# Seven products for eight in part of the first FFN projection of a hybrid decoder layer, and PSUM as one pool

## The chip, the cores and the metric

One core of a Trainium2 chip. The metric is the device time of one execution, in microseconds; runs of the same kernel on the same chip are compared. Engines are TensorE (PE, with its weight loads as PEld), VectorE (DVE), ScalarE (ACT), GpSimd (POOL) and SyncE (SP), which issues the loads.

## What is computed

One layer of a decoder trunk on 256 rows of width 2048, all in float32: a conditioned norm, one wide input projection, two token mixers (an RG-LRU and a windowed attention), gated output projections, and then the part that matters here:

```python
h2 = modulate(rms_norm(x, norm2_g[l]), sh2, sc2)
gate, up = jnp.split(h2 @ w_ffn_in[l], 2, axis=-1)     # 2048 -> 2 x 5632
x = x + g2 * ((jax.nn.silu(gate) * up) @ w_ffn_out[l]) # 5632 -> 2048
```

## The kernel before, in words

**Precision.** A float32 product is made of three matmuls in a reduced type. Each weight block and each activation is split in a high and a low part, and `mm3` (line 346) issues high by high, high by low and low by high into one PSUM bank. ScalarE makes the high part of a weight block (`do_hi`, line 295, the copy at line 301), VectorE the low part (`do_lo`, line 306, the subtraction at line 313).

**Items.** All projections are one list of `Item`s. A normal item is one load of 128x1024 weights (two k-tiles of 128 by 512 columns) with twelve matmuls of 512 columns: two k-tiles, two blocks of 128 rows, three each. `step(i)` (line 323) fixes the order on every queue by hand: first one stage of each open epilogue (`run_posts`, the list `posts`), then the load of item i+5, the making of item i+4 where its weights are computed and not loaded, the high part of i+3, the low part of i+2, then the item's `before` stages, the matmuls of item i, and side work that fits by a planner's clocks (`run_sides`: the costs `T_PE`, `T_DVE`, `T_ACT`, `T_DMA` in line 69). High parts have four buffers, low parts three, loads five, so the low part of i+2 can start only when the matmuls of item i-1 are done. The last four items (`keep=True`) hold their parts in another pool and are free of that.

**First FFN projection** (`add_slab`, line 352, called at lines 1153 to 1155): for each of 11 slabs of 512 hidden columns, first the gate slab (tiles `fg`), then the factor slab (`fu`), each over 16 k-tiles in eight items, into two banks, one for each block of rows. `gate_f_post` (line 1113) applies SiLU behind the gate slab; `up_f_post` (line 1121) multiplies, turns the result by eight transposes (`turned`, line 887), and splits it in parts for the last projection.

**Last projection** (`seven`, line 1206): for eight pairs of k-tiles (`SEVEN`, line 64) a block product of 2x2 blocks (two blocks of rows, two k-tiles, two blocks of columns) is made of seven products where eight would do it plainly. Sums of activation blocks (`f_sum`) and differences of weight blocks (`first` and `second`, lines 1234 and 1243) are needed; four sums of products (`p`, `q`, `r`, `u`) are shared by the pairs and added up once at the end (`combined`, line 1259). It runs in two sweeps; a pair is four items: two loads and two items whose weights VectorE makes.

**PSUM.** Two pools of four banks: `ps_w` for slabs, `ps_m` for the rest, the latter counted by `used["m"]`.

**Around them.** `second_norm` (line 1029) makes the parts of h2 ahead of the first FFN projection, and its `rest` (line 1084) finishes them as an epilogue, one stage for each item. `ada_rows` (line 606) is side work: the last modulation, 32 multiply-adds on VectorE (line 623) into the tile `pa`, and four copies through PSUM (line 629). Behind the last item `finish_first` and `finish_last` (lines 1343 and 1372) end the kernel.

Of the kernel before, what the change touches and what calls it, by code (L numbers as in the profile page):

```python
# [9 lines left out]
F32 = mybir.dt.float32  # L10
# [53 lines left out]
SEVEN = tuple(range(6, 36, 4))  # L64
EARLY = NH - 2 * N_HOLD
# [7 lines left out]
def hybrid_layer(  # L73
# [12 lines left out]
    ps_w = ctx.enter_context(tc.tile_pool(name="ps_w", bufs=4, space=PSUM))  # L86
    ps_m = ctx.enter_context(tc.tile_pool(name="ps_m", bufs=4, space=PSUM))
# [178 lines left out]
    class Item:  # L266


        def __init__(self, src, cols, mm, post=None, keep=False, weight=1, used=None, before=()):
            self.src, self.cols, self.mm, self.post, self.keep, self.weight = src, cols, mm, post, keep, weight  # L270

            self.used, self.before = used or cols, list(before)
# [22 lines left out]
    def do_hi(i):  # L295
        cols, keep = items[i].used, items[i].keep
# [4 lines left out]
        nc.scalar.copy(hi[:, :cols], live[i][0][:, :cols])  # L301
        clock["act"] = max(clock["act"], live[i][3])
        charge(0, cols * T_ACT)
        live[i][1], live[i][3] = hi, clock["act"]

    def do_lo(i):
        cols, keep = items[i].used, items[i].keep
# [5 lines left out]
        nc.vector.tensor_tensor(lo[:, :cols], raw[:, :cols], f32(hi[:, :cols]), op=ALU.subtract)  # L313
        clock["dve"] = max(clock["dve"], live[i][3])
        charge(cols * T_DVE, 0)
# [7 lines left out]
    def step(i):  # L323
        it = items[i]
        run_posts()
# [3 lines left out]
        upto("lo", do_lo, i + N_LO)  # L329
        for stage in it.before:  # L330
            charge(*stage())
# [20 lines left out]
    def add_slab(slab, name, act, k0, k1, post, in_rows=False, before=None, late=0):  # L352
# [25 lines left out]
        for a in range(k0, k1, 2):  # L378
# [3 lines left out]
            ))  # L382

# [643 lines left out]
    h2 = {}  # L1027

    def second_norm(banks):
# [54 lines left out]
        def rest():  # L1084
            turn(7)
            for p in range(NK // 2):
# [5 lines left out]
                yield 1.33, 1.4  # L1092

# [27 lines left out]
    def up_f_post(s):  # L1121
        def post(banks):
# [7 lines left out]
            if 4 * s + 2 not in SEVEN:  # L1130
                fh, fl = b4(f"fh{s}", F32R), b4(f"fl{s}", F32R)
                yield from parts_of(pts, fh, fl)
                f_hi[s], f_lo[s] = fh, fl
                return

            fc, fs = b4(f"fc{s}", F32R, (2, 2, S)), b4(f"fs{s}", F32, (8, P))
            nc.scalar.copy(fc[:, 0], pts[0])
            nc.scalar.copy(fs[:, 0:2, :], pts[1][:, :, 0:P])
            nc.scalar.copy(fs[:, 2, :], pts[1][:, 1, P:])
            yield 0, 1.3  # L1140
            nc.vector.tensor_tensor(fc[:, 1], pts[0], f32(fc[:, 0]), op=ALU.subtract)
            a11, a12, a22, a21 = fs[:, 0, :], fs[:, 1, :], fs[:, 2, :], pts[1][:, 0, P:]
            s1, s2, s3, s4 = (fs[:, i, :] for i in range(3, 7))
            nc.vector.tensor_tensor(s1, a21, a22, op=ALU.add)
            nc.vector.tensor_tensor(s3, a21, a11, op=ALU.subtract)
            nc.vector.tensor_tensor(s2, s1, a11, op=ALU.subtract)
            nc.vector.tensor_tensor(s4, a12, s2, op=ALU.subtract)
            free(m=2)
            f_hi[s], f_lo[s], f_sum[4 * s + 2] = fc[:, 0], fc[:, 1], fs
            yield 1.5, 0  # L1150
# [16 lines left out]
    def bank(t, n):  # L1167

        if (t, n) not in fin:
            fin[t, n] = (ps_w if n < 2 else ps_m).tile([P, 512], F32, tag="wm"[n // 2], name=f"pf{t}{n}")  # L1170
# [31 lines left out]

    def seven(k, n, src):
        sweep = n // 2
        made = {}

        def parts_high():  # L1210
            made["hi"] = wp.tile([P, 8, P], F32R, tag="araw", name=f"ah{sweep}_{k}", bufs=N_ADA)
            nc.scalar.copy(made["hi"][:, 0:7, :], f_sum[k][:, 0:7, :])
            return 0, 0.9

        def parts_low():
            made["lo"] = b4(f"al{sweep}_{k}", F32R, (8, P))
            nc.vector.tensor_tensor(
                made["lo"][:, 0:7, :], f_sum[k][:, 0:7, :], f32(made["hi"][:, 0:7, :]), op=ALU.subtract
            )
            return 1.0, 0  # L1220

        def products(*jobs):

            def go(hi, lo):
                for a, c0, to in jobs:
                    if to in "pqru" and k == SEVEN[0]:
                        fin[to] = (ps_m if sweep == 0 else ps_w).tile([P, 512], F32, tag="mw"[sweep], name=f"p{to}{sweep}")
                    ps = fin[to] if to in "pqru" else bank(int(to[0]), n + int(to[1]))
                    l = [made[h][:, a, :] for h in ("hi", "lo")]
                    w = [h[:, c0:c0 + 512] for h in (hi, lo)]  # L1230
                    mm3(ps, l, w, to in "pqru" and k == SEVEN[0], to in "pqru" and k == SEVEN[-1])
            return go

        def first(i):
            x = fin["made"][:, 0:CH]
            a, b = live[i - 2][0], live[i - 1][0]
            made["a"], made["b"] = a, b
            nc.vector.tensor_tensor(x[:, 0:512], a[:, 512:], a[:, 0:512], op=ALU.subtract)
            nc.vector.tensor_tensor(x[:, 512:], a[:, 512:], b[:, 512:], op=ALU.subtract)
# [327 lines left out]
```

## Time and profile before

| | |
|---|---|
| median of 3 runs | 1569.51 us (1569.43 to 1572.74) |
| the profiled execution | 1573.62 us |
| its span in the trace | 1571.5 us |
| granted clock of TensorE, mean | 0.996 of full speed |
| read from memory | 394.73 MB, 254 GB/s over the span |

The span is the part of the profiled execution that the trace shows, 2.1 us less than its time. The profiled execution is 4.1 us above the median. Busy times overlap, since engines run side by side, and a busy TensorE is not one at its peak. An engine's idle time is put down to what ended it.

### The profile page before, as it was taken

Reading aid. Unit: us, or ns where it says so; the run is one execution under the profiler, and the core shown is the slowest. Engines: PE = TensorE matmul, PEld = TensorE weight load, DVE = VectorE, ACT = ScalarE, POOL = GpSimd, SP = SyncE. Lnnn points to the kernel's source line nnn. Section 1 sums busy time; section 2 is a strip of 40 time slices with the busy share of each in tenths; the row PEclk is TensorE's granted clock in tenths of the full one; section 3 lists DMA queues with packets and bytes.
Section 4 is the critical chain, followed back from the end, with each engine's and each line's share of the span. In section 5 each row is a group of like instructions: output and inputs, shape, how many; then the busy total and the mean of one; then the engine's idle time right before and its main releaser. Section 6 shows DMA issues by size and latency. Waiting matters only on the chain.

```text
span 1571.5 us, 21843 instructions
## 1 busy us (share of the span) xinstructions
PE 1552.6 (99%) x8103; PEld 1332.7 (85%) x8103; DVE 1219.9 (78%) x1589; ACT 798.8 (51%) x1018; POOL 3.8 (0%) x9
## 2 busy tenths in 40 slices
PE   8999999999999999999999999999999999999997
PEld 7999999998878778888888887888888888888886
DVE  7889989899988888998558985545555544998997
ACT  4654443767855455444446444444444444665664
POOL 0000000000000000000000000000000000000000
PEclk9999999999999999999999999999999999999998
DMA  9999997665877897999867997666666666766562
GB/s 367 345 319 337 339 317 271 220 234 167 289 263 256 289 328 278 348 349 307 286 222 241 335 341 241 180 192 191 191 190 188 188 189 211 254 204 212 194 211 107
DMA packets 112908, 400.36 MB, mean 255 GB/s; under 512 B 12433, under 2 KB 12577, under 8 KB 112417
## 3 DMA queue, kind: packets, MB, share of 16 engines
q1 hardware_dynamic: 112514, 398.46, 75.0%
q8 instruction: 63, 1.03, 0.3%
q10 hardware_dynamic: 288, 0.52, 0.1%
q14 instruction: 43, 0.35, 0.1%
HBM read 394.73 MB, written 4.20 MB: 254 GB/s over the span
## 4 chain that ended last, share of the span: by engine, by line
PE 94%; DMA 3%; DVE 2%; ACT 0%; issue 0%; SPq 0%; DVEq 0%; ACTq 0%
PE pf L1194 9%; PE wi L350 6%; PE wi L348 6%; PE wi L349 6%; PE fu L348 5%; PE fu L350 5%; PE fu L349 5%; PE fg L348 5%; PE fg L350 5%; PE fg L349 5%; PE wga L350 2%; PE wga L349 2%; PE wo L348 2%; PE wga L348 2%; PE wo L349 2%; PE wa L349 2%
## 5 line engine op out<-in xcount | busy, mean ns | idle before, releaser
L301 ACT CAST hi<-raw 128x1024 fp32r<-128x1024 f32 (+1 forms) x540 | 554.0, 1027 | 646.0 <-PE fu L350 141.8
L313 DVE TENSOR_TENSOR lo<-raw,hi 128x1024 fp32r<-128x1024 f32 (+1 forms) x540 | 640.1, 1191 | 285.3 <-PE fu L349 91.1
L348 PE MATMUL wi<-h_both,hi 128*128 128x256 f32 x800 | 228.1, 285 | 1.6 <-ACT acc L523 1.6
L350 PE MATMUL wi<-h_both,lo 128*128 128x256 f32 x800 | 227.3, 284 | 2.0 <-DVE lo L313 2.0
L349 PE MATMUL wi<-h_both,hi 128*128 128x256 f32 x800 | 226.9, 284 | 0.0
L350 PEld LDWEIGHTS wi<-h_both,lo 128*128 128x128 f32 x800 | 154.2, 193 | 2.4 <-DVE lo L313 2.4
L348 PEld LDWEIGHTS wi<-h_both,hi 128*128 128x128 f32 x800 | 154.2, 193 | 2.0 <-ACT acc L523 1.8
L349 PEld LDWEIGHTS wi<-h_both,hi 128*128 128x128 f32 x800 | 154.2, 193 | 0.2
L348 PE MATMUL fg<-hi,h_both 128*128 128x512 f32 x352 | 138.4, 393 | 0.1
L348 PE MATMUL fu<-hi,h_both 128*128 128x512 f32 x352 | 137.8, 391 | 0.0
L350 PE MATMUL fg<-hi,h_both 128*128 128x512 f32 x352 | 137.1, 390 | 0.0
L349 PE MATMUL fg<-lo,h_both 128*128 128x512 f32 x352 | 137.0, 389 | 0.0
L350 PE MATMUL fu<-hi,h_both 128*128 128x512 f32 x352 | 137.0, 389 | 0.0
L349 PE MATMUL fu<-lo,h_both 128*128 128x512 f32 x352 | 136.9, 389 | 0.0
L434 DVE CUSTOM_DVE_ANT_0 aw<-aw,crow,vec 128x1024 f32<-128x1024 f32 x79 | 100.6, 1279 | 5.9 <-DMA aw<-in_ada_t_dram 5.8
L434 DVE CUSTOM_DVE_ANT_0 aw<-aw,crow,modc 128x1024 f32<-128x1024 f32 x79 | 101.0, 1281 | 4.3 <-DMA aw<-in_ada_t_dram 4.2
L349 PEld LDWEIGHTS fu<-lo,h_both 128*128 128x128 f32 x352 | 66.1, 188 | 14.1 <-issue 0.5
L348 PEld LDWEIGHTS fu<-hi,h_both 128*128 128x128 f32 x352 | 66.1, 188 | 14.1 <-issue 0.5
L350 PEld LDWEIGHTS fg<-hi,h_both 128*128 128x128 f32 x352 | 66.1, 188 | 14.0 <-DVE h_both L1079 0.2
L350 PEld LDWEIGHTS fu<-hi,h_both 128*128 128x128 f32 x352 | 66.1, 188 | 13.8
L348 PEld LDWEIGHTS fg<-hi,h_both 128*128 128x128 f32 x352 | 66.1, 188 | 13.7 <-ACT h_both L1074 0.3
L349 PEld LDWEIGHTS fg<-lo,h_both 128*128 128x128 f32 x352 | 66.1, 188 | 13.5 <-issue 0.2
(293 smaller groups left out, 2624.9 us busy)
## 6 DMA issues: line engine op xcount, KB each, us to landing
raw<-in_w_f_dram SPq DMA_DIRECT2D x176, 512.0 KB, 3.7
raw<-in_w_in_dram SPq DMA_DIRECT2D x164, 512.0 KB, 6.9
aw<-in_ada_t_dram SPq DMA_DIRECT2D x158, 512.0 KB, 6.5
raw<-in_w_f2a_dram SPq DMA_DIRECT2D x44, 512.0 KB, 3.8
raw<-in_w_f2d_dram SPq DMA_DIRECT2D x36, 512.0 KB, 4.3
raw<-in_w_lru_dram SPq DMA_DIRECT2D x32, 512.0 KB, 6.8
raw<-in_w_att_dram SPq DMA_DIRECT2D x32, 512.0 KB, 7.9
raw<-in_w_o_dram SPq DMA_DIRECT2D x32, 512.0 KB, 4.6
```

Of the source, the lines that this page charges most:

```text
L301: nc.scalar.copy(hi[:, :cols], live[i][0][:, :cols])
L313: nc.vector.tensor_tensor(lo[:, :cols], raw[:, :cols], f32(hi[:, :cols]), op=ALU.subtract)
L348: nc.tensor.matmul(ps, lhsT=lh, rhs=rh, start=start, stop=False, skip_group_check=True)
L349: nc.tensor.matmul(ps, lhsT=lh, rhs=rl, start=False, stop=False, skip_group_check=True)
L350: nc.tensor.matmul(ps, lhsT=ll, rhs=rh, start=False, stop=stop, skip_group_check=True)
L434: nc.vector.tensor_tensor_reduce(out=r, in0=r, in1=crow[:, j * CH:(j + 1) * CH], op0=ALU.mult, op1=ALU.add, scale=1.0, scalar=dst if j els ...
L1194: nc.tensor.matmul(bank(t, n), lhsT=l[:, rows(t)], rhs=w[:, c0:c0 + 512], start=kt == 0 and k == 0, stop=kt == (EARLY - 2 if (t, n) == (1, ...
```

## The change

Three pieces.

1. **Sevens in the first FFN projection.** In slabs 3 to 10 (`SLAB_7`) gate and factor slab become one loop over the eight pairs of k-tiles (`add_pair`). Pairs at k = 4, 8 and 12 (`SEVEN_1`) take seven products for eight; the 2x2 blocks are two blocks of rows, two k-tiles, and as columns the gate block and the factor block. The other five pairs are plain: one item for the gates, one for the factors, twelve matmuls each. A slab holds four banks of its own (row block by gate or factor) and the four shared sums. `shared` reads those behind k = 12 and forms the four values that belong to each bank; `gated_rows` adds them at the slab's end, applies SiLU, multiplies, turns and splits. The sums of activation blocks (`h_sum`) are made once, in twelve more stages of `rest`. Ahead of slab 3 the last modulation is made to finish (`all_modulations`).
2. **PSUM** is one pool of eight banks under one tag.
3. **Order in `step`.** Where the low part that is due belongs to one of the last four items, the open epilogues come behind it and not ahead of it.

The seven of the last projection now goes through the same function `seven` (its order of products and its instructions stay), the four sums through `sums_of`, and the second half of `up_f_post` is now `f_parts`.

```diff
 N_MADE, N_HOLD = 5, 4
 SEVEN = tuple(range(6, 36, 4))
+SEVEN_1, SLAB_7 = (4, 8, 12), 3
...
-    ps_w = ctx.enter_context(tc.tile_pool(name="ps_w", bufs=4, space=PSUM))
-    ps_m = ctx.enter_context(tc.tile_pool(name="ps_m", bufs=4, space=PSUM))
+    ps = ctx.enter_context(tc.tile_pool(name="ps", bufs=8, space=PSUM))
...
+    def sum_bank(name):
+        return ps.tile([P, 512], F32, tag="bank", name=name)
     def wtile(name):
-        return ps_w.tile([P, 2, S], F32, tag="w", name=name)
+        return ps.tile([P, 2, S], F32, tag="bank", name=name)
 
     def mtile(name):
         used["m"] += 1
-        return ps_m.tile([P, 512], F32, tag="m", name=name)
+        return sum_bank(name)
...
+        if not items[min(i + N_LO, len(items)) - 1].keep:
+            run_posts()
         upto("lo", do_lo, i + N_LO)
+        if items[min(i + N_LO, len(items)) - 1].keep:
+            run_posts()
...
+    SUMS = 4
+    def seven(loads, where, act, bank, begin, end, made_in, post=None):
+        got = {}
+        def products(*jobs):
+            def go(hi, lo):
+                for a, c0, to in jobs:
+                    shared = to in "pqru"
+                    w = [h[:, c0:c0 + 512] for h in (hi, lo)]
+                    mm3(bank(to), act(a), w, begin and shared, end and shared)
+            return go
+        def block(k, n):
+            l, c0 = where[k, n]
+            return got[l][:, c0:c0 + 512]
+        def first(i):
+            got.update({0: live[i - 2][0], 1: live[i - 1][0]})
+            x = got["x"] = made_in(0)
+            nc.vector.tensor_tensor(x[:, 0:512], block(0, 1), block(0, 0), op=ALU.subtract)
+            nc.vector.tensor_tensor(x[:, 512:], block(0, 1), block(1, 1), op=ALU.subtract)
+            return x
+        def second(i):
+            y, x = made_in(1), got["x"]
+            nc.vector.tensor_tensor(y[:, 0:512], block(1, 1), x[:, 0:512], op=ALU.subtract)
+            nc.vector.tensor_tensor(y[:, 512:], block(1, 0), y[:, 0:512], op=ALU.subtract)
+            return y
+        plain = ((0, (0, 0), "p"), (1, (1, 0), "00"), (6, (1, 1), "01"))
+        for l in range(2):
+            jobs = [(a, where[kn][1], to) for a, kn, to in plain if where[kn][0] == l]
+            cs = [c0 for _, c0, _ in jobs]
+            items.append(Item(
+                loads[l], CH, products(*jobs), weight=0.25 * len(jobs), used=(min(cs), max(cs) + 512),
+            ))
+        items.append(Item(first, CH, products((3, 0, "r"), (5, 512, "u")), weight=0.5))
+        items.append(Item(second, CH, products((4, 0, "q"), (2, 512, "10")), post, weight=0.5))
+    def sums_of(to, a11, a12, a21, a22):
+        s1, s2, s3, s4 = (to[:, i, :] for i in range(SUMS))
+        nc.vector.tensor_tensor(s1, a21, a22, op=ALU.add)
+        nc.vector.tensor_tensor(s3, a21, a11, op=ALU.subtract)
+        nc.vector.tensor_tensor(s2, s1, a11, op=ALU.subtract)
+        nc.vector.tensor_tensor(s4, a12, s2, op=ALU.subtract)
...
+            for k in SEVEN_1:
+                x = x1T[k // 2]
+                for j in range(2):
+                    nc.scalar.activation(x[:, j, :], x[:, j, :], AF.Identity, bias=modc[:, 3, k + j:k + j + 1])
+                yield 0, 1.0
+                hs = sp.tile([P, 512], F32, tag="t2", name=f"hs{k}").rearrange("p (i n) -> p i n", n=P)
+                sums_of(hs, x[:, 0, rows(0)], x[:, 1, rows(0)], x[:, 0, rows(1)], x[:, 1, rows(1)])
+                yield 1.0, 0
+                h_sum[k] = b4(f"hs{k}", F32R, (2, SUMS, P))
+                nc.scalar.copy(h_sum[k][:, 0], hs)
+                yield 0, 0.6
+                nc.vector.tensor_tensor(h_sum[k][:, 1], hs, f32(h_sum[k][:, 0]), op=ALU.subtract)
+                yield 0.6, 0
...
+    def add_pair(s):
+        banks, v = {}, {}
+        def bank(to):
+            if to not in banks:
+                banks[to] = sum_bank(f"f{to}_{s}")
+            return banks[to]
+        def plain(k, n):
+            def go(hi, lo):
+                for t in range(2):
+                    for kt in (k, k + 1):
+                        c0 = (kt - k) * 512
+                        a = [h[:, rows(t)] for h in h2act(kt)]
+                        mm3(bank(f"{t}{n}"), a, (hi[:, c0:c0 + 512], lo[:, c0:c0 + 512]), kt == 0, kt == NK - 1)
+            return go
+        def act(k):
+            def of_a(a):
+                if a > 2:
+                    return [h_sum[k][:, h, a - 3, :] for h in range(2)]
+                return [h[:, rows(a // 2)] for h in h2act(k + (a > 0))]
+            return of_a
+        def shared():
+            for i in range(2):
+                v[i] = b4(f"v{i}_{s}", F32, (2, 512))
+            g, x = v[0], v[1]
+            nc.scalar.copy(g[:, 0, :], banks["p"])
+            yield 0, 0.6
+            nc.vector.tensor_tensor(x[:, 0, :], banks["q"], g[:, 0, :], op=ALU.add)
+            nc.vector.tensor_tensor(g[:, 1, :], banks["u"], x[:, 0, :], op=ALU.add)
+            yield 1.3, 0
+            nc.vector.tensor_tensor(x[:, 1, :], banks["r"], g[:, 1, :], op=ALU.add)
+            nc.vector.tensor_tensor(x[:, 0, :], banks["r"], x[:, 0, :], op=ALU.add)
+            yield 1.3, 0
+        def gated_rows():
+            g, x = v[0], v[1]
+            for t in range(2):
+                nc.vector.tensor_tensor(g[:, t, :], banks[f"{t}0"], g[:, t, :], op=ALU.add)
+                nc.scalar.activation(g[:, t, :], g[:, t, :], AF.Silu)
+            for t in range(2):
+                nc.vector.tensor_tensor(x[:, t, :], banks[f"{t}1"], x[:, t, :], op=ALU.add)
+            nc.vector.tensor_tensor(x, x, g, op=ALU.mult)
+            free(b4=1)
+            yield 4.0, 1.4
+            yield 0, 0
+            pts = turned(x, f"ft{s}_")
+            free(b4=1)
+            yield 0, 0
+            yield from f_parts(s, pts)
+        start = len(items)
+        for k in range(0, NK, 2):
+            loads = [w_f1[s + 11 * n][:, k * 512:(k + 2) * 512] for n in range(2)]
+            if k in SEVEN_1:
+                last = k == SEVEN_1[-1]
+                seven(
+                    loads, {(0, 0): (0, 0), (1, 0): (0, 512), (0, 1): (1, 0), (1, 1): (1, 512)}, act(k), bank,
+                    k == SEVEN_1[0], last,
+                    lambda i: wp.tile([P, CH], F32, tag="araw", name="made", bufs=N_ADA), shared if last else None,
+                )
+                continue
+            for n in range(2):
+                items.append(Item(loads[n], CH, plain(k, n), gated_rows if (k, n) == (NK - 2, 1) else None))
+        if s == SLAB_7:
+            items[start].before.append(all_modulations)
+    def all_modulations():
+        ada_ffn.finish(streams[-1].fetch)
+        return 0, 0
     for s in range(11):
+        if s >= SLAB_7:
+            add_pair(s)
+            continue
         add_slab(w_f1[s], f"fg{s}", h2act, 0, NK, gate_f_post(s), True)
         add_slab(w_f1[11 + s], f"fu{s}", h2act, 0, NK, up_f_post(s), True)
```

## Rows read from the trace of the kernel before

**Rows 1.** Part 1 of the page: each engine's busy time, share and instructions.

```profile
PE 1552.6 (99%) x8103; PEld 1332.7 (85%) x8103; DVE 1219.9 (78%) x1589; ACT 798.8 (51%) x1018; POOL 3.8 (0%) x9
```

**Rows 2.** The waits of TensorE: total us, times, longest us; two of nine rows.

```profile
PE pf L1194 <- DVE lo L313: 2.0, 1, 2.0
...
PE wi L348 <- ACT acc L523: 1.6, 1, 1.6
```

**Rows 3.** Stretches: length; busy PE, PEld, DVE, ACT, POOL (instructions); granted clock; DMA share; GB/s.

```profile
1100.00:1200.00 100.00, 100.00 (x451) 82.98 (x450) 51.21 (x53) 42.31 (x47) 0.00 (x0) 1.00 0.63 188
...
1400.00:1500.00 100.00, 100.00 (x443) 82.81 (x442) 94.52 (x109) 58.94 (x68) 0.00 (x0) 1.00 0.61 201
```

**Rows 4.** Timeline of TensorE in the first FFN projection, two products twelve apart.

```profile
1085.58 0.39 PE L348 MATMUL fu<-hi,h_both 128*128 128x512 f32 x1
...
1088.30 0.39 PE L348 MATMUL fu<-hi,h_both 128*128 128x512 f32 x1
```

**Rows 5.** Timeline of TensorE in the last projection: one group of sevens, then the next.

```profile
1522.06 0.39 PE L348 MATMUL pp<-hi,ah 128*128 128x512 f32 x1
...
1526.82 0.61 PE L1194 MATMUL pf<-hi,fc 128*128 128x512 f32 x2
...
1532.26 0.39 PE L348 MATMUL pp<-hi,ah 128*128 128x512 f32 x1
```

**Rows 6.** Timeline of VectorE, same stretch: start, us, line, out<-in, [idle before <-releaser].

```profile
1514.33 2.35 DVE L313 TENSOR_TENSOR lo<-raw,hi 128x1024 fp32r<-128x1024 f32 x2
1516.60 0.69 DVE L1238 TENSOR_TENSOR last<-raw 128x512 f32<-128x512 f32 x1
1517.20 0.68 DVE L1239 TENSOR_TENSOR last<-raw,raw 128x512 f32<-128x512 f32 x1
1517.81 0.69 DVE L313 TENSOR_TENSOR lo<-raw,hi 128x512 fp32r<-128x512 f32 x1
1518.41 1.08 DVE L1217 TENSOR_TENSOR al<-fs,ah 128x896 fp32r<-128x896 f32 x1
1519.41 0.69 DVE L1245 TENSOR_TENSOR last<-raw,last 128x512 f32<-128x512 f32 x1
1520.13 0.69 DVE L1246 TENSOR_TENSOR last<-raw,last 128x512 f32<-128x512 f32 x1
1520.74 1.22 DVE L313 TENSOR_TENSOR lo<-raw,hi 128x1024 fp32r<-128x1024 f32 x1
1521.88 1.22 DVE L313 TENSOR_TENSOR lo<-last,hi 128x1024 fp32r<-128x1024 f32 x1
1523.39 1.22 DVE L313 TENSOR_TENSOR lo<-last,hi 128x1024 fp32r<-128x1024 f32 x1 [0.29 <-ACT hi L301]
1524.53 2.35 DVE L313 TENSOR_TENSOR lo<-raw,hi 128x1024 fp32r<-128x1024 f32 x2
```

**Rows 7.** The tile sg: durations min/median/max, first and last start, of SiLU and product.

```profile
L1117 ACT ACTIVATE sg<-fg x22: 593/599/602, 859.9 to 1307.8; 128x512 f32<-128x512 f32 x22
L1125 DVE TENSOR_TENSOR sg<-fu,sg x22: 679/692/692, 881.4 to 1329.6; 128x512 f32<-128x512 f32 x22
```

**Rows 8.** Timeline of VectorE, first projection: the parts of one slab, and what follows.

```profile
984.33 0.69 DVE L1141 TENSOR_TENSOR fc<-ft,fc 128x512 fp32r<-128x512 f32 x1
...
985.90 1.23 DVE L313 TENSOR_TENSOR lo<-raw,hi 128x1024 fp32r<-128x1024 f32 x1
```

**Rows 9.** Costliest groups: TensorE's first product of each gate slab; busy, mean, idle before.

```profile
L348 PE MATMUL fg<-hi,h_both 128*128 128x512 f32 x352 | 138.4, 393 | 0.1
```

**Rows 10.** The tile pa, the last modulation: its sums on VectorE, its copies on TensorE.

```profile
L623 DVE SCALAR_TENSOR_TENSOR pa<-aw,cact,pa x32: 1276/1279/1286, 861.1 to 955.4; 128x1024 f32<-128x1024 f32 x32
...
L629 PE MATMUL pb<-pa,ones x8: 591/592/592, 959.7 to 979.1; 128*128 128x512 f32 x8
```

**Rows 11.** Engines by stretch in the tail, behind TensorE's wait (columns as in rows 3).

```profile
1555.74:1558.94 3.20, 3.20 (x17) 3.20 (x15) 2.41 (x4) 0.67 (x2) 0.00 (x0) 0.50 0.00 0
```

**Rows 12.** Timeline of VectorE at the end: the last sum that waits for TensorE.

```profile
1563.10 0.42 DVE L1293 TENSOR_TENSOR y<-late,pa 128x256 f32<-128x256 f32 x1 [1.40 <-PE late L350]
```

More of the change, by code (lines that the diff above doesn't have):

```diff
@@ L300, in do_hi @@
             hi = wp.tile([P, CH], F32R, tag="hi", name=f"hi{i}", bufs=N_HI)
-        nc.scalar.copy(hi[:, :cols], live[i][0][:, :cols])
+        nc.scalar.copy(hi[:, cs], live[i][0][:, cs])
         clock["act"] = max(clock["act"], live[i][3])
-        charge(0, cols * T_ACT)
+        charge(0, (cs.stop - cs.start) * T_ACT)
         live[i][1], live[i][3] = hi, clock["act"]
     def do_lo(i):
-        cols, keep = items[i].used, items[i].keep
+        cs, keep = items[i].used, items[i].keep
         if keep:
@@ L1129, in post @@
             yield 0, 0
[L1130 to L1140, printed above, removed]
@@ L1169, in bank @@
         if (t, n) not in fin:
-            fin[t, n] = (ps_w if n < 2 else ps_m).tile([P, 512], F32, tag="wm"[n // 2], name=f"pf{t}{n}")
+            fin[t, n] = sum_bank(f"pf{t}{n}")
         return fin[t, n]
@@ L1200, in out_products, with seven_last @@
         return go
-    def seven(k, n, src):
-        sweep = n // 2
-        made = {}
+    def seven_last(k, n, src):
+        parts = {}
         def parts_high():
-            made["hi"] = wp.tile([P, 8, P], F32R, tag="araw", name=f"ah{sweep}_{k}", bufs=N_ADA)
-            nc.scalar.copy(made["hi"][:, 0:7, :], f_sum[k][:, 0:7, :])
+            hi = parts[0] = wp.tile([P, 8, P], F32R, tag="araw", name=f"ah{n}_{k}", bufs=N_ADA)
+            nc.scalar.copy(hi[:, 0:7, :], f_sum[k][:, 0:7, :])
             return 0, 0.9
@@ L1215, in parts_low @@
         def parts_low():
[L1216 to L1219, printed above, removed]
+            lo = parts[1] = b4(f"al{n}_{k}", F32R, (8, P))
+            nc.vector.tensor_tensor(lo[:, 0:7, :], f_sum[k][:, 0:7, :], f32(parts[0][:, 0:7, :]), op=ALU.subtract)
             return 1.0, 0
[L1222 to L1239, printed above, removed]
-            made["x"] = x
-            return x
-        def second(i):
-            y, x, b = fin["made"][:, CH:], made["x"], made["b"]
-            nc.vector.tensor_tensor(y[:, 0:512], b[:, 512:], x[:, 0:512], op=ALU.subtract)
-            nc.vector.tensor_tensor(y[:, 512:], b[:, 0:512], y[:, 0:512], op=ALU.subtract)
-            return y
+        def own(to):
+            if to not in "pqru":
+                return bank(int(to[0]), n + int(to[1]))
+            if k == SEVEN[0]:
+                fin[to] = sum_bank(f"p{to}{n}")
+            return fin[to]
@@ L1249, in seven @@
         items[-3].before.append(parts_high)
         items[-2].before.append(parts_low)
-        half = 0.5
-        items.append(Item(src[k], CH, products((0, 0, "p")), weight=half / 2, used=512))
-        items.append(Item(src[k + 1], CH, products((1, 0, "00"), (6, 512, "01")), weight=half))
-        items.append(Item(first, CH, products((3, 0, "r"), (5, 512, "u")), weight=half))
-        items.append(Item(
-            second, CH, products((4, 0, "q"), (2, 512, "10")), (lambda: combined(n)) if k == SEVEN[-1] else None, weight=half,
-        ))
+        seven(
+            (src[k], src[k + 1]), {(0, 0): (0, 0), (0, 1): (0, 512), (1, 0): (1, 0), (1, 1): (1, 512)},
+            lambda a: [parts[h][:, a, :] for h in range(2)], own, k == SEVEN[0], k == SEVEN[-1],
+            lambda i: fin["made"][:, i * CH:(i + 1) * CH], (lambda: combined(n)) if k == SEVEN[-1] else None,
+        )
@@ L1325, in hybrid_layer @@
             if k in SEVEN:
-                seven(k, n, src)
+                seven_last(k, n, src)
                 continue
```

38 lines of the change are left out of this document (22 added, 16 removed).

## The prediction

> **What bounds the kernel now.** I read the page's part 1 first: TensorE is busy 99% of the span, VectorE 78%, ScalarE 51% [rows 1]. Busy alone is weak evidence, so the waits of TensorE come next. There are nine kinds, some 10 us together in 1571.5; the two that matter here are one of 2.0 us in the last projection and one of 1.6 us for a bank near the start [rows 2]. The rest of the span TensorE spends issuing products, so time goes away where products go away, as long as nothing else becomes late. In the stretch that changes, from 1100 to 1200 us, VectorE is busy 51%, ScalarE 42%, the loads 63% [rows 3]; in the last projection, which has sevens already, VectorE is busy 94.5% and TensorE still all the time [rows 3].
>
> The price of a product is its distance to the next, not its duration (0.39 us, since they overlap): twelve start in 2.72 us, 0.2267 us each [rows 4]. In the last projection, 21 products of a seven take 1526.82 - 1522.06 = 4.76 us, the same 0.2267, and a seven with its plain pair 10.20 us, 45 times 0.2267, without a gap [rows 5]. So a product with summed operands costs no more than a plain one, and the seven's items can feed TensorE.
>
> **Products removed.** A plain pair over gates and factors has eight block products of three matmuls, 24; a seven has 21. Three pairs in eight slabs: 3 x 3 x 8 = 72 products fewer, 72 x 0.2267 = **16.3 us**. A slab takes (1307.8 - 859.9) / 10 = 44.8 us now [rows 7]; it should take 44.8 - 9 x 0.2267 = 42.7. The eight transposes stay.
>
> **What hides the new work.** VectorE, one slab, by distances of starts [rows 6]. A plain item's low part: 1.14, ten of them, 11.4 us. A seven: from 1516.60 to 1524.53 are 7.93 us; off go the 1.00 of the line-1217 operation, which splits activation sums and has no part here (they are split once, ahead), and the 0.29 idle: 6.64, three of them 19.9. `shared`: four additions of 512, 0.60 each, 2.4. `gated_rows`: four more and a product of 1024 (priced as a low part, 1.14), 3.5. The parts: 985.90 - 984.33 = 1.6 [rows 8]. Sum 38.8 us in 42.7, 91%, less than the last projection bears at 94.5%. ScalarE: 42% of 44.8 is 19 us; each seven adds one and a half high parts and `shared` one copy, 5.5 instructions a slab; at today's mean of 42.31 / 47 = 0.90 us [rows 3] that is 5 us, so 24 of 42.7. Loads: 16 of 512 KB a slab as before, in the same queue past nothing new; their share rises from 0.63 to 0.66. So these cost nothing; if VectorE's cover went, each slab would pay what exceeds 42.7 us.
>
> **The slab's end** is the tight place, since SiLU, sums and product now fall together. Let T be the end of the slab's last product. In step order VectorE can make the low part of the next slab's second item from T - 2.72, when TensorE starts the slab's last item; it is done at T - 1.58. Then come the last two sums of `shared` (1.2, to T - 0.38), the four additions of `gated_rows` (three of their banks are complete by then, the fourth at T; to T + 2.0), its product (to T + 3.2; SiLU's two calls of 0.60 [rows 7] run beside the additions), and the low part of the next slab's third item, to T + 4.3. TensorE wants that one after two items, at T + 5.44. The slack is 1.1 us. With full durations instead of starts (0.69 and 1.22) the same chain ends at T + 5.1, still in time. I take nothing; upper bound 1 us in each of eight slabs, 8 us.
>
> **Banks.** The next slab starts on four banks while its predecessor's own four are still to be read; the shared four are free (read by T - 0.4 at the latest). The two transposed tiles take two of the others at the third item (T + 5.4), the next shared sums the rest from the fifth (T + 12), when the additions have long read them. I take nothing. Elsewhere one pool changes no count, since four and four were the most in use; the one wait for a bank is worth 1.6 us [rows 2], so from -1.6 to +1.6 us, taken as nothing.
>
> **Activation sums and the last modulation.** Per seven pair one subtraction and four sums of 128 columns, the same mix as above at 1.6 us [rows 8]: 4.7 us on VectorE, and some 4 us on ScalarE, in twelve steps of slab 0. There the last modulation is running (32 operations of 1.28 us between 861.1 and 955.4 [rows 10]); the planner puts it back by as much. Slab 3 starts near 859.9 + 3 x 44.8 - 22 = 972, so the 32 end 15 us early now, and 5 us later is in time. Its four copies end at 979.1 [rows 10], hence two or three are forced at slab 3's start; the same TensorE work at another moment. Nothing, with 6 us as the upper end if operations of the 32 were left over.
>
> **The tail.** The 2.0 us wait is a low part of the last item that stands behind four additions on VectorE. The new order in `step` puts it ahead of them. TensorE's wait goes, and so should the low clock behind it: for 3.20 us the granted clock was 0.50, the 1.2 GHz level [rows 11], after the engine had stood still; that is another 1.6 us. But VectorE is late next: it works without pause through the tail and waits only 1.40 us for TensorE's last product [rows 12]. So the end moves by 1.4 us, not 3.6. Bounds: nothing, and 1.4. I take 1.4.
>
> **Sum.** 16.3 + 1.4 = 17.7 us. The profiled execution took 1573.62, so 1555.9 on its scale; the median of the runs is 4.1 lower, and from it 1569.51 - 17.7 = **1551.8 us**, 1.1% less.
>
> **Rivals.**
>
> *The bank comes late (the other side).* If the pool hands a slab's first tile the bank that was released last in the order of the program, that is the one the fourth addition reads, TensorE stands until T + 2.0 at each of eight starts: 16 us, the whole gain: 1568, no change. A stop of 2.0 us was followed by half clock for 3.20 us [rows 11]; if that repeats, 1.4 to 1.6 us more each, 12 us: 1580, slower. It decides between 0 and 2 us of wait in the first product of each slab. For it: a slab holds all eight banks. Against it: today, too, a slab's first bank is taken when the previous slab's banks have just been given to SiLU or the product, and the first product of 352 in the gate slabs waited 0.1 us in all [rows 9]; the pool hands out one that has been free longer. Chance 0.06 for no change and 0.06 for slower. The Trainium skill, "Perfetto Trace Analysis", section "Optimization Strategy", says that a gap repeating on the engine that should be saturated can mean too little PSUM for the next tile; by that this rival would hold; the trace shows no such gap with half the banks in a slab [rows 9].
>
> *VectorE late at the slab's end.* If each hop of the chain above costs more than its start distance, the slack of 1.1 us goes and each start stalls 0.5 to 1 us: 1556 to 1560. For it: seven operations in a row with SiLU between them. Against it: in the last projection VectorE idles 0.29 in 10.2 us and TensorE not at all [rows 5, 6]. Chance 0.10.
>
> *The last modulation late.* Two of its 32 operations left at slab 3, with their loads 2.9 us apart ((955.4 - 861.1) / 32 [rows 10]): 6 us, 1558. Against it are the 15 us of room. Chance 0.04.
>
> **How the numbers follow.** The forecast has 0.74; its own range is 1549 to 1556 (a bank wait of 1.6 less and some hundredths per slab more). Together with the two small rivals faster has 0.88; same and slower 0.06 each. A measurement of this kernel can tell 0.2%, some 3 us, from no change, and all these cases are clear of it but the 1568. The range 1549 to 1560 leaves the bank rivals out, and little else.
>
> **What the changed profile would show.** Starts of SiLU in slabs 3 to 10 42.7 us apart; 72 products fewer on TensorE; VectorE some 91% busy there; no wait of TensorE at slab starts; no 2.0 us wait in the tail and no low clock behind it; VectorE's last wait for TensorE gone. Waits of TensorE for additions on banks would prove the first rival, waits for low parts at each slab's third item the second. The forecast fails if slabs are not 2 us shorter.

## The result, and the profile after

The changed kernel took 1554.01 us, the median of 6 runs (1551.7 to 1556.62); the kernel before took 1570.74 beside it, the median of 6 (1568.68 to 1575.41). The ratio is 0.9892, 95% interval 0.9873 to 0.9911: faster by 1.1%, against 1551.8 us and 17.7 / 1569.51 = 1.1% forecast. In the profiled executions the span fell from 1571.5 to 1553.4 us, 18.1 less; the medians differ by 16.7, and executions of one kernel spread over 5 to 7 us.

Part 1 of the page of the changed kernel answers to [rows 1]:

```profile
PE 1534.8 (99%) x8031; PEld 1318.1 (85%) x8031; DVE 1359.0 (87%) x1804; ACT 843.8 (54%) x1083; POOL 3.9 (0%) x9
```

72 products fewer, as counted. TensorE is still busy 99%; VectorE did 139 us more work and ScalarE 45, beside it. The three longest of TensorE's six kinds of wait (in us: total, times, longest) answer to [rows 2]:

```profile
PE wi L357 <- DVE lo L317: 3.4, 2, 2.0
PE wl L356 <- DVE lo L317: 1.5, 1, 1.5
PE w L627 <- DVE hx L1590: 1.1, 1, 1.1
```

All lie ahead of the first FFN projection. No wait is named for a bank or a low part at a slab's start, and the 2.0 us one in the last projection is gone. The tile `v` (durations min/median/max, first and last start) gives the period of a slab by its one product of gates and factors, and stretches of about a slab show who is busy in it (columns as in [rows 3]):

```profile
L1272 DVE TENSOR_TENSOR v<-v,v x8: 1225/1226/1226, 1018.4 to 1315.0; 128x1024 f32<-128x1024 f32 x8
```

```profile
1058.95:1101.40 42.45, 42.45 (x193) 35.21 (x193) 39.43 (x49) 24.08 (x29) 0.00 (x0) 1.00 0.60 200
1101.40:1143.90 42.50, 42.50 (x193) 35.30 (x192) 39.50 (x49) 24.14 (x29) 0.00 (x0) 1.00 0.60 199
```

One in each of eight slabs, so seven periods: (1315.0 - 1018.4) / 7 = 42.37 us. TensorE has no idle time in the two stretches; VectorE's reserve is 42.5 - 39.5 = 3 us. Periods of the kernels below are taken from the same row of theirs.

**Where the 18.1 us came from.** The tail, from the second copy of the shared sum `pp` to the start of the last sum that takes a product of TensorE, was 1563.1 [rows 12] - 1536.8 = 26.3 us and is 1545.0 - 1520.2 = 24.8: 1.5 us. The first SiLU [rows 7] starts at 859.5 instead of 859.9: 0.4. The remaining 16.2 lie between them, against 72 x 0.2267 = 16.3.

VectorE at the seam of two slabs, in the changed kernel's timeline, is what the eight starts hang on (start, duration, line, out<-in):

```profile
1141.73 0.68 DVE L1261 TENSOR_TENSOR v<-fr,v 128x512 f32<-128x512 f32 x1
1142.34 0.68 DVE L1262 TENSOR_TENSOR v<-fr,v 128x512 f32<-128x512 f32 x1
1142.93 1.28 DVE L1268 TENSOR_TENSOR v<-f,v 128x512 f32<-128x512 f32 x2
1144.13 1.28 DVE L1271 TENSOR_TENSOR v<-f,v 128x512 f32<-128x512 f32 x2
1145.51 1.23 DVE L1272 TENSOR_TENSOR v<-v,v 128x1024 f32<-128x1024 f32 x1
1146.65 2.35 DVE L317 TENSOR_TENSOR lo<-raw,hi 128x1024 fp32r<-128x1024 f32 x2
```

and TensorE in the same place:

```profile
1143.28 0.39 PE L355 MATMUL f<-hi,h_both 128*128 128x512 f32 x1
...
1148.73 1.03 PE L954 MATMUL ft<-ident,v 128*128 128x128 f32 x8
1149.52 0.48 PE L355 MATMUL f<-hi,h_both 128*128 128x512 f32 x1
1149.83 0.40 PE L356 MATMUL f<-lo,h_both 128*128 128x512 f32 x1
```

Let T be 1143.28, the start of the next slab's first product. Shared sums, additions and product run to T + 3.37 (the start of what follows them), and the first low part of the row of two (the next slab's third item) is done some 1.2 later, at T + 4.5. The product at 1149.83, T + 6.55, is the first that reads it: the eight transposes and one high product stand ahead of it. The room was 2.0 us.

### The profile page after: what moved, and what is told of

It is laid out like the page before. It is cut to its first block, busy times and chain, and to the rows that moved or that the text cites. A ratio compares the mean times of both kernels' runs of the same rounds, so it can differ in the third digit from the quotient of the medians.

```text
span 1553.4 us, 22040 instructions
## 1 busy us (share of the span) xinstructions
PE 1534.8 (99%) x8031; PEld 1318.1 (85%) x8031; DVE 1359.0 (87%) x1804; ACT 843.8 (54%) x1083; POOL 3.9 (0%) x9
## 4 chain that ended last, share of the span: by engine, by line
PE 94%; DMA 3%; DVE 2%; issue 0%; ACT 0%; SPq 0%; DVEq 0%; ACTq 0%
PE pf L1345 9%; PE wi L357 6%; PE wi L356 6%; PE wi L355 6%; PE f L357 6%; PE f L356 6%; PE f L355 6%; PE wga L356 2%; PE wga L357 2%; PE wga L355 2%; PE wo L355 2%; PE wo L356 2%; PE wa L356 2%; PE wa L355 2%; PE wa L357 2%; PE wo L357 2%
## 5 line engine op out<-in xcount | busy, mean ns | idle before, releaser
L317 DVE TENSOR_TENSOR lo<-raw,hi 128x1024 fp32r<-128x1024 f32 (+1 forms) x540 | 622.6, 1165 | 114.2 <-issue 45.0
L355 PE MATMUL f<-hi,h_both 128*128 128x512 f32 x368 | 144.3, 392 | 0.0
L357 PE MATMUL f<-hi,h_both 128*128 128x512 f32 x368 | 143.2, 389 | 0.0
L356 PE MATMUL f<-lo,h_both 128*128 128x512 f32 x368 | 143.2, 389 | 0.0
L305 ACT CAST hi<-made 128x1024 fp32r<-128x1024 f32 x48 | 50.7, 1057 | 90.7 <-PE f L357 86.4
L357 PEld LDWEIGHTS f<-hi,h_both 128*128 128x128 f32 x368 | 69.1, 188 | 14.4
L356 PEld LDWEIGHTS f<-lo,h_both 128*128 128x128 f32 x368 | 69.1, 188 | 14.3 <-issue 0.2
L355 PEld LDWEIGHTS f<-hi,h_both 128*128 128x128 f32 x368 | 69.1, 188 | 14.3 <-ACT hi L305 0.2
L317 DVE TENSOR_TENSOR lo<-made,hi 128x1024 fp32r<-128x1024 f32 x48 | 58.8, 1225 | 20.5 <-PE f L356 17.3
L1345 PE MATMUL pf<-hi,fc 128*128 128x512 f32 x256 | 71.0, 389 | 0.0
L305 ACT CAST hi<-last 128x1024 fp32r<-128x1024 f32 x32 | 33.8, 1055 | 53.9 <-PE pf L1345 52.2
L1345 PEld LDWEIGHTS pf<-hi,fc 128*128 128x128 f32 x256 | 48.0, 188 | 9.9
L355 PE MATMUL wl<-hi,yh 128*128 128x512 f32 x128 | 52.5, 410 | 0.0
```

Source lines behind the costliest of these rows:

```text
L305: nc.scalar.copy(hi[:, cs], live[i][0][:, cs])
L317: nc.vector.tensor_tensor(lo[:, cs], raw[:, cs], f32(hi[:, cs]), op=ALU.subtract)
L355: nc.tensor.matmul(ps, lhsT=lh, rhs=rh, start=start, stop=False, skip_group_check=True)
L356: nc.tensor.matmul(ps, lhsT=lh, rhs=rl, start=False, stop=False, skip_group_check=True)
L357: nc.tensor.matmul(ps, lhsT=ll, rhs=rh, start=False, stop=stop, skip_group_check=True)
L1345: nc.tensor.matmul(bank(t, n), lhsT=l[:, rows(t)], rhs=w[:, c0:c0 + 512], start=kt == 0 and k == 0, stop=kt == (EARLY - 2 if (t, n) == (1, ...
```

## The experiments

Ratios are times over the kernel before on the same chip, with 95% intervals; the changed kernel stands at 0.9892.

**Are the sevens the gain?** Pool, order and all new code stay, no slab uses a seven:

```diff
-SEVEN_1, SLAB_7 = (4, 8, 12), 3
+SEVEN_1, SLAB_7 = (), 11
```

> The changed kernel with no sevens in the first FFN projection: all 11 slabs as before, no sums of activation blocks; one pool and the new order in step stay. My theory (72 products are the gain): 1.4 us under the kernel before, ratio 0.999, slabs 44.5 us apart. Rival (the one pool takes waits away elsewhere): more than 5 us under the kernel before, with fewer waits of TensorE ahead of the first FFN projection.

Measured: 1571.82, ratio 0.9998 [0.9990, 1.0007]; 8103 products again, 44.8 us a slab again by the first and last starts of [rows 7] ((1306.1 - 858.1) / 10), a tail of 24.8, and TensorE's early waits as in the changed kernel. The whole measurable gain is the sevens'. One pool and the new order without them gained nothing that the times can tell; the sevens need the one pool, since a slab of theirs holds all eight banks.

**The tail, from both sides.** The new order in the kernel before, and the old order in the changed kernel:

```diff
 # kernel before
-        run_posts()
+        if not items[min(i + N_LO, len(items)) - 1].keep:
+            run_posts()
         upto("lo", do_lo, i + N_LO)
+        if items[min(i + N_LO, len(items)) - 1].keep:
+            run_posts()
```

> The kernel before with the new order in step alone. My theory: the 2.0 us wait of TensorE in the tail and the low clock behind it go, but VectorE is late next, and the end comes 1.4 us earlier (ratio 0.999). Rival (TensorE sets the end): 3.6 us earlier, 2.0 of wait and 1.6 of clock.

> The changed kernel with the old order in step. My theory: the wait of 2.0 us and the half clock are back in the tail, and the end comes 1.4 us later than in the changed kernel. Rival (the tail is another one now that the slabs are shorter): no wait in the tail, same time as the changed kernel.

Measured: the first took 1571.92, ratio 0.9999 [0.9990, 1.0008], with a tail of 1559.0 - 1534.2 = 24.8 us, no 2.0 us wait and a granted clock of 1.00 in it. The second took 1556.18, ratio 0.9898 [0.9885, 0.9912], with a tail of 1545.0 - 1518.7 = 26.3. Its waits of TensorE, its stretches and VectorE's timeline bring back what [rows 2, 11, 12] showed:

```profile
PE pf L1342 <- DVE lo L317: 2.0, 1, 2.0
```

```profile
1537.00:1538.00 1.00, 1.00 (x4) 0.81 (x3) 1.00 (x2) 0.00 (x0) 0.00 (x0) 0.50 0.00 0
```

```profile
1545.05 0.42 DVE L1412 TENSOR_TENSOR y<-late,pa 128x256 f32<-128x256 f32 x1 [1.27 <-PE late L354]
```

So the order is worth 1.5 us by the trace in both pairs. The times can't tell it: in the profiled executions of these kernels the first SiLU alone, ahead of which little differs, starts anywhere from 856.1 to 861.7 us.

**More sevens: what would have stopped them.** A fourth seven saves 3 x 0.2267 = 0.68 us of TensorE a slab, and by the prediction's prices costs VectorE 6.64 - 2 x 1.14 = 4.4: 43.2 us in 41.8. Two placements:

```diff
-SEVEN_1, SLAB_7 = (4, 8, 12), 3
+SEVEN_1, SLAB_7 = (2, 6, 10, 12), 3
```

> The changed kernel with four pairs of eight by seven products (k = 2, 6, 10, 12). TensorE has three products less in a slab, 0.68 us, VectorE 6.64 - 2.28 = 4.36 us more, 38.8 + 4.4 = 43.2 us against 41.8 of TensorE. My theory (the 91% is nearly all that VectorE can give): VectorE becomes the bound, slabs 43 us or more apart against 42.5, 5 us or more slower than the changed kernel, and TensorE waits for low parts. Rival (VectorE has room left): 8 x 0.68 = 5.4 us faster than the changed kernel.

```diff
-SEVEN_1, SLAB_7 = (4, 8, 12), 3
+SEVEN_1, SLAB_7 = (4, 6, 10, 12), 3
```

> Four pairs by seven products at k = 4, 6, 10 and 12 in place of 2, 6, 10 and 12, all on VectorE: the pair behind the slab's end is plain again. With k = 2 the slabs came 45.1 us apart, and TensorE waited 1.1 us at each slab's second shared sum for a bank that VectorE had still to read. Theory A (the clump at the slab's end cost what goes beyond VectorE's sum): slabs 43.2 to 43.8 us apart, 6 to 11 us slower than the changed kernel. Theory B (VectorE's sum alone, whatever the order): 45 us again, 20 us slower.

Measured: the first 1573.76, ratio 1.0018 [1.0009, 1.0028], slabs of (1333.9 - 1018.7) / 7 = 45.03 us; the second 1567.30, ratio 0.9968 [0.9958, 0.9978], slabs of (1327.2 - 1018.6) / 7 = 44.09. TensorE's waits in the two, then one slab of each:

```profile
PE fu L355 <- DVE fc L1220: 7.1, 7, 1.1
...
PE fr L356 <- DVE lo L317: 2.5, 15, 0.2
PE f L356 <- DVE lo L317: 2.2, 8, 0.3
```

```profile
PE f L356 <- DVE lo L317: 4.4, 16, 0.3
...
PE fr L356 <- DVE lo L317: 2.7, 16, 0.2
```

```profile
1061.90:1107.10 45.20, 43.44 (x191) 34.28 (x190) 43.33 (x55) 25.52 (x31) 0.00 (x0) 1.00 0.56 188
```

```profile
1059.00:1103.00 44.00, 43.12 (x189) 34.08 (x188) 42.93 (x55) 25.36 (x30) 0.00 (x0) 1.00 0.58 194
```

With a seven at k = 2 a product into the shared bank `fu` waits 1.0 us in each of seven slabs: its bank was a transposed tile's, which VectorE reads last in line 1220. From k = 4 on it does not, and 45.03 - 44.09 = 0.94 us is about that. What is left are low parts: VectorE is busy 42.9 of 44.0 us, and TensorE waits for it in small pieces, 0.9 us a slab. 44.09 lies between the 43.2 to 43.8 of theory A and the 45 of theory B, nearer to A. It is more than either engine needs by itself, 42.9 on VectorE and 42.37 - 0.68 = 41.7 on TensorE. A fourth seven lost time in both places, so three are as many as VectorE carries here.

**Could GpSimd carry the differences?** The four sevens of the second placement, with the first two differences of each on GpSimd (lines 418 and 419; `eng` is a new argument of `seven`, here GpSimd's `tensor_tensor`, and VectorE's in the last projection):

```diff
-            nc.vector.tensor_tensor(x[:, 0:512], block(0, 1), block(0, 0), op=ALU.subtract)
-            nc.vector.tensor_tensor(x[:, 512:], block(0, 1), block(1, 1), op=ALU.subtract)
+            eng(x[:, 0:512], block(0, 1), block(0, 0), op=ALU.subtract)
+            eng(x[:, 512:], block(0, 1), block(1, 1), op=ALU.subtract)
```

> Four pairs by seven products (k = 4, 6, 10, 12) and the first two of the four weight differences of each seven in the first FFN projection on GpSimd, which is idle. VectorE: 43.2 - 4 x 1.2 = 38.4 us a slab against 41.8 of TensorE. My theory, if GpSimd works beside VectorE: no waits, slabs 41.8 us apart, 5.4 us faster than the changed kernel. Rival: GpSimd's operations with two operands in SBUF keep VectorE's from theirs, so its subtractions become longer or wait (the Trainium skill, SBUF — State Buffer, section on the two sides of it, states a port pair shared by the two and locked for a whole instruction; by that VectorE loses more than the 4.8 us it is spared, since GpSimd is the slower): slabs over 43 us apart, slower than the changed kernel.

Measured: 1595.63, ratio 1.0145 [1.0130, 1.0160], slabs of (1355.8 - 1023.6) / 7 = 47.46 us. The tile `made` (min/median/max ns):

```profile
L317 DVE TENSOR_TENSOR lo<-made,hi x64: 1214/1218/2322, 986.6 to 1343.7; 128x1024 fp32r<-128x1024 f32 x64
L418 POOL TENSOR_TENSOR made<-raw,raw x32: 1290/1330/2289, 971.9 to 1336.4; 128x512 f32<-128x512 f32 x32
L419 POOL TENSOR_TENSOR made<-raw x32: 1277/2268/2280, 973.1 to 1338.5; 128x512 f32<-128x512 f32 x32
L424 DVE TENSOR_TENSOR made<-raw,made x32: 676/682/1780, 981.4 to 1339.6; 128x512 f32<-128x512 f32 x32
```

A subtraction that takes VectorE 0.68 us takes GpSimd 1.28 to 2.29, and VectorE's own low part goes from 1.22 to as much as 2.32 us, longer by 1.1. The lengthening is on both sides, and these durations fit each standing still while the other works. Three low parts in a row take 5.69 us, where two without GpSimd beside them take 2.35:

```profile
1071.02 5.69 DVE L317 TENSOR_TENSOR lo<-raw,hi 128x1024 fp32r<-128x1024 f32 x3
```

The Trainium skill, "SBUF — State Buffer", section "SBUF: two separate sides", describes it: GpSimd, where it reads SBUF, and a VectorE operation with two operands in SBUF share a pair of ports that one of them holds for a whole instruction. The trace agrees: VectorE's operations that grew here, L317 and L424, read two operands in SBUF. So an engine that is idle on the page is no reserve for VectorE where both need that pair.

Not all of the loss is GpSimd's. In five of the slabs the granted clock fell to 0.50 for some 3 us behind a wait of some 1.4 us for a low part; one stretch of it:

```profile
1153.00:1156.00 3.00, 3.00 (x8) 2.32 (x7) 2.80 (x3) 2.16 (x3) 0.00 (x0) 0.50 0.83 283
```

The periods grow from 46.27 and 46.97 us in the two ahead of it to 47.50 and then 47.84 to 47.87. So up to some 1.6 us a slab may be the clock's; the first, 46.27 against 44.09 without GpSimd, has no low clock in it.

**The bank rival, made true.** Each slab's own four banks are kept for all slabs. In the first kernel every second slab uses them in reversed order, so that a slab's first product meets the bank that the fourth addition reads; in the second the order stays, so that it meets the one that the first addition reads:

```diff
-            if to not in banks:
+            if to not in banks and to in "pqru":
                 banks[to] = sum_bank(f"f{to}_{s}")
+            elif to not in banks:
+                i = ("00", "10", "01", "11").index(to)
+                if len(own) < 4:
+                    own.append(sum_bank(f"own{i}"))
+                banks[to] = own[3 - i if (s - SLAB_7) % 2 else i]
```

(`own` is a list made once; the second kernel has `own[i]` in the last line.)

> The changed kernel with four fixed banks for a slab's own sums, handed to the next slab in reverse order, so that its first product goes to the bank that the last of the four additions reads. The rival of the prediction, made real: TensorE stands from T to about T + 2.1 at seven of eight slab starts, 15 us; if the clock falls to half for some 3 us behind each stop, as in the tail before, 11 us more. My theory: 15 to 26 us slower than the changed kernel; the clock tells which. Rival (VectorE catches up in the stop, and later waits shrink by as much): under 5 us slower.

> The same four fixed banks in the same order in each slab, so that the first product goes to the bank that the first addition reads. My theory: the first addition ends 0.3 us behind T, so TensorE waits 0.3 to 0.5 us at seven slab starts, 2 to 4 us in all, no half clock. Rival (any bank of the slab before costs the full chain of additions): as the kernel with the reversed order.

Measured: the first 1572.90, ratio 1.0011 [0.9999, 1.0023], slabs of (1331.9 - 1016.9) / 7 = 45.00 us; the second 1556.94, ratio 0.9910 [0.9895, 0.9925], slabs of (1316.8 - 1016.2) / 7 = 42.94. TensorE's waits in the first, then two stretches of it, one behind the first stop and one behind the fourth:

```profile
PE own L355 <- DVE v L1278: 14.7, 7, 2.1
```

```profile
1018.00:1020.00 2.00, 2.00 (x10) 1.66 (x9) 1.45 (x3) 0.00 (x0) 0.00 (x0) 1.00 0.00 0
...
1153.00:1154.00 1.00, 1.00 (x3) 0.76 (x3) 0.59 (x1) 0.00 (x0) 0.00 (x0) 0.50 0.00 0
```

and in the second:

```profile
PE own L355 <- DVE v L1275: 2.2, 7, 0.3
```

The rival's mechanism is right: TensorE waits 2.1 us at each of seven starts, and that one choice of bank is worth the whole gain. Its half clock came behind one stop of the seven, the fourth: six periods are 44.73 to 44.77 us, the one with the low clock 46.37. So a stop costs 44.76 - 42.37 = 2.4 us and the half clock 1.6 more where it comes. In the second kernel a start costs 0.57 us, in all about the 2 to 4 us that were expected; the times alone can't tell it from the changed kernel. In the changed kernel the banks that the pool handed out were free in time: TensorE shows no wait there. The Trainium skill, "Perfetto Trace Analysis", section "Optimization Strategy", says that the same gap repeating on the engine that should be saturated can mean too little SBUF or PSUM for the next tile. The 2.1 us at each start are such a gap; here the number of banks is the same in both kernels, and the order in which they come again makes the difference.

**How much room has VectorE at the seam?** One or three additions of 1024 columns, 1.22 us each, are put behind line 1272 (the diff shows one); nothing reads their results:

```diff
             nc.vector.tensor_tensor(x, x, g, op=ALU.mult)
+            for _ in range(1):
+                nc.vector.tensor_tensor(g, x, x, op=ALU.add)
             free(b4=1)
```

> The changed kernel with one more addition of 1024 (about 1.14 us, its result unused) on VectorE at the end of each slab of the sevens, behind the product with SiLU. By the profile of the changed kernel the low part of the next slab's third item is done 4.5 us behind T and wanted at 6.5, since the eight transposes come first. My theory: 2.0 us of room, so no wait and the time of the changed kernel. Rival (room of 1.1 us as the prediction had it, or less): 0 to 0.3 us a slab, up to 2 us.

> The same with three such additions, 3.4 us a slab. My theory (room of 2.0 us): TensorE waits 1.4 us for a low part at each slab's third item, 8 x 1.4 = 11 us slower than the changed kernel, more if the clock falls. Rival (room of 1.1 us): 2.3 us a slab, 18 us. Rival (only the sum over a slab counts: 38.8 + 3.4 = 42.2 of 42.5 us): no slower.

Measured: with one 1553.13, ratio 0.9889 [0.9872, 0.9905], slabs of (1313.3 - 1016.4) / 7 = 42.41 us, no wait in them; with three 1573.43, ratio 1.0019 [1.0009, 1.0029], slabs of (1329.5 - 1014.9) / 7 = 44.94. The waits of TensorE with three, one of them in its timeline, and a slab:

```profile
PE f L356 <- DVE lo L317: 11.9, 7, 1.7
...
PE fr L356 <- DVE lo L317: 1.7, 6, 0.3
```

```profile
1063.10 1.03 PE L954 MATMUL ft<-ident,v 128*128 128x128 f32 x8
1063.89 0.48 PE L355 MATMUL f<-hi,h_both 128*128 128x512 f32 x1
1066.07 0.50 PE L356 MATMUL f<-lo,h_both 128*128 128x512 f32 x1 [1.71 <-DVE lo L317]
```

```profile
1058.10:1103.10 45.00, 42.99 (x193) 35.11 (x191) 42.77 (x52) 24.00 (x29) 0.00 (x0) 1.00 0.56 188
```

One addition (1.14 us from start to start) is free, so the room is at least that. Three (3.7 us) exceed 2.0 by 1.7, and that is the wait at the third item: the room of 2.0 is right, that of 1.1 is not, and the sum over a slab alone doesn't decide. The loss against the changed kernel, 1.0019 - 0.9892 = 0.0127 of the time, is still some 20 us, and not the 11 that went with this theory. A slab pays 44.94 - 42.37 = 2.6: the stop of 1.7, a second one of 0.3 at the next seven (`fr`), and about 0.3 more for each stop (last section). VectorE is not busy all the time in that slab, 42.8 of 45.0 us.

**One slab earlier.**

```diff
-SEVEN_1, SLAB_7 = (4, 8, 12), 3
+SEVEN_1, SLAB_7 = (4, 8, 12), 2
```

> The changed kernel with the sevens from slab 2 on, nine slabs in place of eight. My theory (the last modulation must be done ahead of them): slab 2 starts near 927 us, when some ten of the 32 sums of the modulation are still to come (they end at 955), and its copies on TensorE stand in front of the slab's first product. At 1.3 us a sum on VectorE TensorE waits 13 us, at the pace of its loads (2.95 us a sum) 28; less 2.0 us for the three sevens more: 11 to 26 us slower than the changed kernel. Rival (the planner draws the sums forward or TensorE does other work): 2 us faster.

Measured: 1569.36, ratio 0.9981 [0.9971, 0.9992], some 14 us more than the changed kernel. TensorE's timeline at the start of slab 2, and two stretches:

```profile
939.09 5.25 PE L691 MATMUL pb<-pa,ones 128*128 128x512 f32 x8 [15.96 <-issue]
```

```profile
926.00:930.00 4.00, 0.00 (x0) 0.00 (x0) 4.00 (x5) 0.00 (x0) 0.00 (x0) 0.50 0.63 203
...
940.00:944.00 4.00, 4.00 (x9) 1.77 (x7) 0.28 (x1) 1.66 (x3) 0.00 (x0) 0.72 0.10 42
```

The last modulation's sums run to 939 there, and TensorE stands 16.0 us; the granted clock is 0.50 in the middle of the stop and 0.72 in the stretch of the copies behind it. The sevens of one more slab give 2.0 back: about 14. Slab 2 is too early, slab 3 is not.

**VectorE at the end.** In the changed kernel VectorE's timeline in the tail has no wait for TensorE left:

```profile
1542.39 0.16 DVE L1469 TENSOR_REDUCE st<-ss 128x1 f32<-128x4 f32 x1 [0.85 <-ACT y L1424]
1542.91 0.16 DVE L1471 RECIPROCAL r<-r 128x1 f32<-128x1 f32 x1 [0.36 <-ACT r L1462]
...
1544.96 0.42 DVE L1415 TENSOR_TENSOR y<-late,pa 128x256 f32<-128x256 f32 x1
```

TensorE's last product starts at 1542.34, yet its sum at 1544.96:

```profile
1542.34 0.28 PE L357 MATMUL late<-hi,fl 128*128 128x256 f32 x1
```

VectorE is late, after two waits for ScalarE. If so, a sum drawn into its idle 0.85 us brings the end forward:

```diff
     def finish_first():
         for _ in residual(0, 3):
             pass
+        fin["y"], _ = add_block(1, fin["late", 0], 1536, 256)
...
-        y, _ = add_block(1, fin["late", 0], a, 256)
+        y = fin["y"]
```

> The changed kernel with the last row block's first sum (the two operations of 0.42 us on the first half of the last columns) drawn ahead of the end of row block 0 on VectorE, where VectorE waits 0.85 us for ScalarE. My theory (VectorE sets the end of the changed kernel): the end comes 0.85 us earlier, 23.9 us in place of 24.8 from the copy of the sum p to the last of the two sums, too little for the times to tell from the changed kernel (0.05%), ratio 0.9885 to 0.9895. Rival (TensorE's last product or ScalarE sets the end): no shorter.

Measured: 1552.67, ratio 0.9876 [0.9860, 0.9893]. In VectorE's timeline the sum fills the gap, and the 0.85 is gone:

```profile
1543.61 0.42 DVE L1415 TENSOR_TENSOR y<-late,pa 128x256 f32<-128x256 f32 x1
1544.06 0.43 DVE L1417 TENSOR_TENSOR last<-y,last 128x256 f32<-128x256 f32 x1
1544.54 0.16 DVE L1470 TENSOR_REDUCE st<-ss 128x1 f32<-128x4 f32 x1
...
1546.33 0.42 DVE L1415 TENSOR_TENSOR y<-late,pa 128x256 f32<-128x256 f32 x1
```

The tail is 1546.3 - 1522.3 = 24.0 us instead of 24.8. So VectorE did set the end. By the trace this tail is shorter than those of both kernels; the time can't be told from the changed kernel's.

## Why the prediction was right, and where it was not

**Products removed: right.** 72 fewer at 0.2267 us, with no gap between them; without sevens the time is that of before. The period was forecast 42.7 and is 42.37. The 44.8 from which it was worked out, ten periods at once, held the copies of the last modulation, which stand in one period only. A period behind them, from ScalarE's timeline of the kernel before, is 1084.42 - 1040.01 = 44.41, and 44.41 - 2.04 = 42.37:

```profile
1040.01 0.60 ACT L1117 ACTIVATE sg<-fg 128x512 f32<-128x512 f32 x1 [0.30 <-PE fg L350]
...
1084.42 0.60 ACT L1117 ACTIVATE sg<-fg 128x512 f32<-128x512 f32 x1 [0.30 <-PE fg L350]
```

The sum of 16.3 was not touched by that.

**VectorE's cover: right, a little thinner.** Forecast 38.8 us in 42.7, 91%; measured 39.4 to 39.5 busy in 42.45, 93%. ScalarE's 24 came as 24.1. The loads moved 199 GB/s instead of 188, as fewer microseconds for the same bytes must, but their share went to 0.60, not up to 0.66: the share of [rows 3] doesn't scale with the rate.

**The slab's end: right in its result, mis-sized in its slack.** The chain of VectorE came within 0.2 us of its forecast (product to T + 3.37 instead of T + 3.2). What was wrong is "TensorE wants that one after two items, at T + 5.44": the eight transposes and the third item's first, high, product come first, so it is wanted at T + 6.55, and the slack is 2.0 us, not 1.1. One added operation free and a wait of 1.7 us with three fit 2.0. The term was taken as nothing, so the mis-sizing did not reach the sum.

**Banks: right, and the rival's half clock was overpriced.** No wait appeared. Made true, the rival costs 2.4 us a slab, more than its 2.0, and ends at a ratio of 1.0011, the "no change" of its milder form. The half clock, taken over from the one place in [rows 11], came behind one stop in seven in the profiled execution: 1.6 us in place of 12. "1580, slower" would need it behind every stop.

**Sums of activations and last modulation: right.** The 32 operations of `pa` start between 860.8 and 955.1, as in [rows 10], so the 5 us by which the planner was to put them back did not come; the last ends 17 us ahead of slab 3's first product (973.3), as the room of 15 us said. One slab earlier they are late and cost 14 us, so the rival was real, and the choice of slab 3 is what keeps it away.

**The tail: right.** Forecast 1.4, measured 1.5 in two pairs; the wait and the low clock went, and VectorE is late instead. It does not work "without pause through the tail", though: it waits 0.85 and 0.36 us for ScalarE, and the sum drawn into the first of these shortened the end by 0.8.

## What to carry to other kernels

Where TensorE issues without a gap, a product removed is worth its pitch, and the question is whether the engines beside it still fit the shorter stage: here three sevens fit with 3 us of VectorE to spare and a fourth lost 12 to 20 us against the changed kernel. Check the seam of two stages by what each product reads, in the order of issue (the room was twice what counting whole items gave), and ask which bank comes next as well as how many there are. A wait taken off TensorE at the end of a kernel is worth only what the next late engine leaves of it.

## What the runs showed of the hardware that was not expected

**The clock behind a short stop.** A stop of 2.0 us in the tail is followed by a granted clock of 0.50, the 1.2 GHz level, in the kernel before [rows 11] and again with the old order in the changed kernel. Of seven stops of 2.1 us at slab starts, all behind the same products, one is followed by 0.50, from some 1.5 us behind the restart and for 3.2 us, and six by 1.00, the 2.4 GHz level. With GpSimd, waits of only 1.4 us were followed by 0.50 in five slabs, and by 1.00 in the two ahead of them; with three additions all seven waits of 1.7 us were followed by 1.00. So neither the length of the stop nor the products ahead of it set these cases apart; what does stays open.

**What a stop costs.** Each of these stops cost about 0.3 us more than the wait that the profile names: 2.39 for 2.10 with the reversed banks (without the slab of the half clock), 0.57 for 0.31 with the banks in order, 2.57 for 1.71 and 0.30 together with three additions. The wait is counted from the end of the product before it, but in an unbroken stream the next product starts 0.39 - 0.23 = 0.16 us ahead of that end, and the first products behind a stop lie further apart (1066.41 - 1066.07 = 0.34 us in place of 0.23).

**GpSimd beside VectorE.** 32 pairs of subtractions on an engine that was idle made the kernel 1595.63 - 1567.30 = 28 us slower than the same four sevens without it, of which up to some 8 us (five slabs, 1.6 each) may be the low clock's.

**No cheap excess.** With four sevens VectorE has 42.9 us of work in a slab and TensorE 41.7, yet the slab took 44.09, 1.2 more than the longer of the two: each still waits for the other now and then (TensorE 0.9 us in a slab, VectorE idle 1.1 of 44.0).
